# Down projection of a gated ConvFFN: eight block products become seven (Strassen-Winograd), two at a time with the depth outermost

## The chip, the cores and the metric

The kernel runs on one core of a Trainium2 chip. The metric is the device time of one execution in microseconds (us). The names of the engines are those of the profile: PE is the matrix engine (PEld its weight loads), DVE the vector engine, ACT the scalar engine, POOL the general engine, SP the engine whose queue issues all DMAs here. SBUF is the memory on the core, PSUM the accumulators' memory, of 8 banks of 128x512 fp32 numbers.

## The reference

The reference is one layer of a decoder with three sub-layers: two token mixers side by side, cross-attention to 256 memory tokens, and a gated ConvFFN. Each is normalised before and after (RMSNorm) and added to the residual stream. There are 1024 tokens, 1024 features, and 2816 hidden features in the ConvFFN. The change is in the last product and what follows it:

```python
def conv_ffn(h, w_up, conv_w, conv_b, w_down):
    a = causal_depthwise_conv(h @ w_up, conv_w, conv_b)
    val, gate = jnp.split(a, 2, axis=-1)
    return (val * jax.nn.gelu(gate)) @ w_down        # (1024 x 2816) @ (2816 x 1024)
...
        f = conv_ffn(h, w_up[l], conv_w[l], conv_b[l], w_down[l])
        x = x + rmsnorm(f, g_ffn_post[l])
```

## The kernel before

Everything is kept with features on the partitions and tokens along the free axis; tokens come in two halves of 512, h = 0 and h = 1. An fp32 product is made of three fast products: each operand is split into a rounded part and a rest (`hi`, `lo`), and `mm3` (L227) issues hi x hi, hi x lo and lo x hi into one bank. So each 128x512 operand costs an ACT cast (`hi`) and a DVE subtraction (`lo`), in `split` (L250) for activations and in `Stream.split_to` (L117) for weights, which are loaded as 128x512 tiles tagged `raw`.

The gated hidden features come out of the up projection as 22 blocks of 128 (`NP`), for each token half, and are written to DRAM (`fd[k][h]`, L1215). The up projection is itself done by Strassen's scheme in its second part; its last products are those of block 21, in the order of `TURN` (L61): S2, S1, S3, 22 and S4.

`down` (L1346) then computes the output's 8 feature blocks of 128. `sweep(h, done)` (L1352) takes one token half: for each of the 22 depth blocks it loads the hidden block (`get_f`, L1337), splits it, and adds three matmuls to each of seven banks. The eighth block has no bank during the sweep. `last` (L1366) computes it afterwards from the hidden parts that are still in SBUF, in one go for h = 0 and by two quarters of 256 tokens for h = 1. The first half's statistics and output (`finish`, L755) run beside the second sweep, a step at a time. The second half ends by quarters: statistics of the first quarter (`rms`, L273) and their broadcast (`bcast`, L300) are taken while the last quarter's matmuls run (`steps1`, at the depth blocks `TAIL_R` and `TAIL_B`), and its output is finished by `finish_pair` (L771) on DVE and POOL. After the last matmul come the square, the statistics, the broadcast and the output of the last quarter.

`rms` has PE sum the squares over partitions (L278), then 11 small DVE operations for the inverse root; `bcast` has PE spread the result (L305) and ACT copy it to SBUF (L308).

A scheduler sets the order of each engine's instructions when the program is built: it simulates the program and takes the ready instruction that was written first. Each engine then works through its own list in order, and waits at an instruction until that one's inputs are there and its buffer is free. From `self.pinned = True` (L1424) on, marked instructions keep the program's order among themselves; those that are not marked (those of `finish` are not) go where the simulation finds them ready. Buffers have tags with a fixed number of slots (L54 to L58): `w` 13 (weight parts), `b` 32, `raw` 4, `f` 20, `fr` 4, `rs` 4.

## Time and profile before

| | us |
|---|---|
| median of three timed runs (lowest, highest) | 1372.89 (1370.04, 1375.63) |
| the profiled execution | 1373.9 |
| its span, first to last instruction | 1372.2 |
| last matmul of the last product ends, in the span | 1355.8 |
| PE busy, share of the span | 1301.2 (95%) |
| DVE, ACT, POOL busy | 979.4, 618.6, 543.3 |
| mean granted PE clock | 0.971 |

A row of a timeline gives the start, the length, the engine, the line of the kernel, the operation, output <- inputs, shapes and count; in brackets stands how long the engine had waited and for what. "x24" merges 24 instructions in a row. A row of stretches gives, from A to B, each engine's busy time and count, the PE clock, the DMA engines' busy share and the rate in GB/s.

### The profile page before, as it was taken

How to read it: one execution, taken by the hardware profiler on the slowest of the kernel's cores; microseconds unless marked ns; L12 is line 12 of the kernel's file. 1: busy time of each engine (PE TensorE's matmuls, PEld its weight loads, DVE VectorE, ACT ScalarE, POOL GpSimd, SP SyncE). 2: the span in 40 equal slices, each digit the busy share in tenths (PEclk: the TensorE clock that was granted, in tenths of full speed). 3: DMA queues.
4: the chain of work that ended last, by engine and by line, in shares of the span. 5: the costliest groups of instructions: out<-in, count | busy, mean ns of one | idle time of the engine just before them, and what ended most of it. 6: DMA issues, size and time to landing. Idle time of an engine off the chain costs nothing. (4 is left out here: it accounts for less than half of the span.)

```text
span 1372.2 us, 19095 instructions
## 1 busy us (share of the span) xinstructions
PE 1301.2 (95%) x6418; PEld 1100.4 (80%) x6418; DVE 979.4 (71%) x1605; ACT 618.6 (45%) x1155; POOL 543.3 (40%) x433
## 2 busy tenths in 40 slices
PE   9799898779998999889999999999999999999995
PEld 8688897778887888778887788888888888887885
DVE  7968788876376547785577978888898884257225
ACT  7223331245444445444545545555555564253232
POOL 1576345834245005530544568666564110020002
PEclk9899999889999999999999999999999999999997
DMA  9644326346335214442376685545453176356431
GB/s 314 188 145 133 94 72 174 88 140 199 99 119 161 68 48 131 154 154 70 102 231 213 193 279 172 161 154 164 143 169 122 60 251 206 96 149 220 144 114 62
DMA packets 136259, 204.20 MB, mean 149 GB/s; under 512 B 32096, under 2 KB 47328, under 8 KB 136160
## 3 DMA queue, kind: packets, MB, share of 16 engines
q1 hardware_dynamic: 136160, 202.98, 47.8%
q8 instruction: 50, 0.82, 0.3%
q14 instruction: 49, 0.40, 0.1%
HBM read 156.41 MB, written 42.32 MB: 145 GB/s over the span
## 5 line engine op out<-in xcount | busy, mean ns | idle before, releaser
L233 PE MATMUL acc<-b,w 128*128 128x512 f32 (+1 forms) x2496 | 593.7, 391 | 7.7 <-DVE b L730 4.0
L233 PEld LDWEIGHTS acc<-b,w 128*128 128x128 f32 x2496 | 465.0, 191 | 104.6 <-DVE b L730 6.1
L134 DVE TENSOR_TENSOR w<-raw,w 128x512 fp32r<-128x512 f32 (+2 forms) x306 | 261.4, 860 | 208.5 <-PE acc L233 129.3
L131 ACT CAST w<-raw 128x512 fp32r<-128x512 f32 x328 | 198.3, 607 | 242.4 <-PE acc L233 129.3
L233 PE MATMUL sx<-b,w 128*128 128x512 f32 x912 | 220.8, 393 | 1.9 <-ACT T L1275 1.9
L233 PEld LDWEIGHTS sx<-b,w 128*128 128x128 f32 x912 | 172.9, 190 | 38.5 <-ACT T L1275 2.3
L710 POOL TENSOR_TENSOR ac<-ac,sq 128x512 f32<-128x512 f32 x49 | 74.9, 1537 | 289.5 <-ACT sq L709 246.2
L233 PE MATMUL acc<-T,w 128*128 128x512 f32 x528 | 127.0, 389 | 0.0
L233 PEld LDWEIGHTS acc<-T,w 128*128 128x128 f32 x528 | 99.1, 188 | 20.5
L724 POOL TENSOR_TENSOR m<-m,rs 128x512 f32<-128x512 f32 x32 | 50.1, 1570 | 61.4 <-DMA rs<-x1d 17.0
L233 PE MATMUL sx<-T,w 128*128 128x512 f32 x264 | 66.5, 389 | 0.0
L233 PEld LDWEIGHTS sx<-T,w 128*128 128x128 f32 x264 | 49.6, 188 | 10.3
L709 ACT ACTIVATE sq<-m 128x512 f32<-128x512 f32 x63 | 39.6, 632 | 28.3 <-POOL m L724 14.2
L774 POOL TENSOR_TENSOR m<-m,st 128x512 f32<-128x512 f32 x3 | 4.8, 1591 | 117.9 <-ACT st L308 117.9
L233 PE MATMUL acc<-w,b 128*128 128x256 f32 x384 | 50.9, 290 | 0.0
L1214 POOL TENSOR_TENSOR b<-b,m 128x512 f32<-128x512 f32 x22 | 31.5, 1434 | 46.1 <-ACT m L1213 45.7
L233 PEld LDWEIGHTS acc<-w,b 128*128 128x128 f32 x384 | 48.4, 197 | 0.1
L115 POOL TENSOR_TENSOR st<-st,b 128x512 f32<-128x512 f32 x20 | 26.4, 1319 | 54.3 <-DMA st<-in_w_up 39.2
L134 DVE TENSOR_TENSOR w<-b,w 128x512 fp32r<-128x512 f32 x40 | 42.1, 1052 | 7.7 <-issue 4.9
L134 POOL TENSOR_TENSOR w<-raw,w 128x512 fp32r<-128x512 f32 x22 | 30.4, 1383 | 41.8 <-ACT w L131 22.7
L723 DVE SCALAR_TENSOR_TENSOR m<-m,gains,st 128x512 f32<-128x512 f32 x32 | 38.3, 1262 | 5.6 <-ACT st L308 5.6
L1200 ACT ACTIVATE m<-acc,conv 128x512 f32<-128x512 f32 x44 | 34.4, 782 | 15.1 <-DVE acc L1319 11.9
(333 smaller groups left out, 2056.8 us busy)
## 6 DMA issues: line engine op xcount, KB each, us to landing
raw<-in_w_up SPq DMA_DIRECT2D x68, 256.0 KB, 2.9
raw<-in_w_dk SPq DMA_DIRECT2D x44, 256.0 KB, 2.7
fr<-fd SPq DMA_DIRECT2D x41, 256.0 KB, 4.0
b<-in_w_up SPq DMA_DIRECT2D x40, 256.0 KB, 2.8
raw<-in_w_dk SPq DMA_DIRECT2D x44, 192.0 KB, 2.5
raw<-in_w_out SPq DMA_DIRECT2D x32, 256.0 KB, 2.7
raw<-in_w_q SPq DMA_DIRECT2D x32, 256.0 KB, 2.8
raw<-in_w_o SPq DMA_DIRECT2D x32, 256.0 KB, 2.7
```

Of the source, the lines that this page charges most:

```text
L115: g.tensor_tensor(p["S4"], p["12"], p["S2"], ALU.subtract)
L131: nc.scalar.copy(hi[:, :w], t[:, :w])
L134: e.tensor_tensor(lo[:, :w], t[:, :w], hi[:, :w], ALU.subtract)
L233: self.pin(nc.tensor.matmul(ps, lhsT=x, rhs=y, start=first and i + j == 0, stop=last and i == n - 1 and j == 2, skip_group_check=go_on))
L709: nc.scalar.activation(sq, src, AF.Square)
L710: (e or nc.gpsimd).tensor_tensor(acc, acc, sq, ALU.add)
L723: v.scalar_tensor_tensor(x, x, self.gain[gpost][:, i:i + 1], bc, ALU.mult, ALU.mult)
L724: g.tensor_tensor(x, x, rs, ALU.add)
L774: self.pin(e.tensor_tensor(x, x, bc, ALU.mult))
L1200: nc.scalar.activation(t, src, AF.Identity, bias=self.cw(blk, 3), scale=self.cw(blk, 2))
L1214: nc.gpsimd.tensor_tensor(val, val, gate, ALU.mult)
```

## The change

The output's features are cut into two halves of four blocks, the tokens into their halves, and the depth of 22 blocks into two halves of 11 (k and k + 11). Winograd's form of Strassen's scheme makes the 2x2 block product from seven products of 11 depth blocks. They are done in four phases; in the first three, two products run at a time in 2 x 4 banks (`A` and `B`), with the depth outermost:

- Phase 0: weights "11" by hidden "a" into A, "12" by "b" into B. Their sum is the final x11 (first four feature blocks, second token half).
- Phase 1: S2 by T2, added on into A, and S1 by T1 into B anew.
- Phase 2: S3 by T3, added on into A, and S4 by "d" added on into B. What A and B hold at the ends of phases 1 and 2 is combined on ACT and DVE into x12 and x22 (all eight blocks of the first token half).
- Phase 3: weights "22" by T4, added on into A, which then holds the last four blocks of the second token half. It runs by quarters: all 11 depth steps for 256 tokens, then for the other 256 tokens block by block.

S1 to S4 are sums and differences of weight blocks, T1 to T4 of hidden blocks. They are made per depth step by `d_sums` on 128x512 tiles: T1 on DVE, the others on POOL. Each is then split like any operand. T2 and S2 stay in SBUF until T4 and S4 are made from them. `d_prep` keeps loads, sums and splits ahead of the matmuls; the shared weight stream no longer serves this product.

A depth step of phases 0 to 2 has 24 matmuls of 512 columns, 4 splits and 4 or 5 loads of 256 KB. Phase 1 adds 3 sums on POOL and one on DVE per step, phase 2 adds 3 on POOL, and phase 3 one on POOL. In all there are 33 x 24 = 792 matmuls of 512 columns and 264 of 256, where before there were 990 and 132.

The first token half's squares, statistics and output (`first_half`) can start only after phase 2, and so run beside phase 3; the quarters' statistics are placed at `TAIL_R` = (0, 7) and `TAIL_B` = (1, 4), which are block and depth step of the last quarter.

```diff
-TAIL_R = 5
-TAIL_B = 10
+TAIL_R = (0, 7)
+TAIL_B = (1, 4)
 T_FROM = 11
 T_RATE = 1
 FETCH = 2
-OUT_RATE = 1
-F_AHEAD = 3
-F_FIRST = {"S1": 1, "S3": 2, "22": 3}
+D_LOAD = 2
+D_FIRST = {"S3": 1, "22": 2}
 SLOTS = {"b": 32, "m": 16, "w": 13, "st": 3, "ac": 2, "sq": 2, "raw": 4}
 SLOTS_1 = {"k": 15, "x": 14}
 SLOTS_2 = {"kv": 16, "t": 11, "rs": 2}
 SLOTS_3 = {"T": 24, "rs": 2, "t": 3}
-SLOTS_4 = {"f": 20, "fr": 4, "rs": 4}
+SLOTS_4 = {"f": 21, "fr": 4, "rs": 4}
 BANKS = {"acc": 4, "sx": 3, "st": 1}
...
-        for h in range(2):
-            for k in range(NP):
-                ids["dn"][h, k] = [w.add(a["w_dk"][k][:, c:c + n].unsqueeze(1)) for c, n in ((0, 512), (512, 384))]
-            ids["d7"][h] = [w.add(a["w_d7"][:, k:min(k + 4, NP)]) for k in range(0, NP, 4)]
...
-                if i == NP - 1 and name in F_FIRST:
-                    self.get_f(F_FIRST[name], "t")
+                if i == NP - 1 and name in D_FIRST:
+                    self.d_prep(D_FIRST[name])
...
-    def get_f(self, n, tag="fr"):
-        while len(self.f) < min(n, 2 * NP):
-            h, k = divmod(len(self.f), NP)
-            t = self.slot(tag)
-            self.nc.sync.dma_start(t, self.fd[k][h])
-            hl = self.f[h, k] = self.pair("b" if 0 <= k - 4 * h < 16 else "f")
-            self.split(*hl, t)
+    def d_load(self, n):
+        nc = self.nc
+        ph, k = divmod(n, 11)
+        s = self.ds[k]
+        def get(key, src, tag):
+            s[key] = self.slot(tag)
+            nc.sync.dma_start(s[key], src)
+        w = lambda o, j: self.a["w_dk"][k + 11 * j][:, HALF * o:HALF * o + HALF]
+        x = lambda j, h: self.fd[k + 11 * j][h]
+        if ph == 0:
+            get("11", w(0, 0), "b")
+            get("12", w(0, 1), "raw")
+            get("a", x(0, 1), "t" if n < 2 else "f")
+            get("b", x(1, 1), "t" if n < 2 else "fr")
+        elif ph == 1:
+            if k < 2:
+                get("a", x(0, 1), "f")
+            get("21", w(1, 0), "f")
+            get("22", w(1, 1), "b")
+            get("c", x(0, 0), "f")
+            get("d", x(1, 0), "f")
+        elif ph == 2:
+            get("11", w(0, 0), "b")
+            get("21", w(1, 0), "f")
+            get("12", w(0, 1), "raw")
+            get("c", x(0, 0), "f")
+            get("d", x(1, 0), "f")
+        else:
+            get("22", w(1, 1), "raw")
+            get("b", x(1, 1), "fr")
+    def d_sums(self, n):
+        v, g = self.nc.vector, self.nc.gpsimd
+        ph, k = divmod(n, 11)
+        s = self.ds[k]
+        def sub(key, to, x, y, e=g, op=ALU.subtract):
+            e.tensor_tensor(s[to], s[x], s[y], op)
+            s[key] = s[to]
+        if ph == 1:
+            sub("S1", "22", "21", "22", g, ALU.add)
+            sub("S2", "11", "S1", "11")
+            sub("T1", "c", "c", "a", v)
+            sub("T2", "a", "d", "T1")
+        elif ph == 2:
+            sub("S3", "21", "11", "21")
+            sub("S4", "S2", "12", "S2")
+            sub("T3", "c", "d", "c")
+        elif ph == 3:
+            sub("T4", "b", "b", "T2")
+    def d_split(self, n):
+        ph, k = divmod(n, 11)
+        s = self.ds[k]
+        names = (("11", "a", "12", "b"), ("S2", "T2", "S1", "T1"), ("S3", "T3", "S4", "d"), ("22", "T4"))[ph]
+        for i, key in enumerate(names):
+            if i % 2 == 0:
+                tag = "w" if ph < 3 or k < 6 else "b"
+            else:
+                tag = "b" if ph < 3 or k >= 8 else "f"
+            hl = self.dp[n, i] = self.pair(tag)
+            self.split(*hl, s.pop(key) if key not in ("S2", "T2", "11", "a", "d") else s[key])
+    def d_prep(self, n):
+        while self.n_prep < min(n, 44):
+            i = self.n_prep
+            while self.n_load <= min(i + D_LOAD, self.d_last):
+                self.d_load(self.n_load)
+                self.n_load += 1
+            while self.n_sums <= min(i + 1, 43):
+                self.d_sums(self.n_sums)
+                self.n_sums += 1
+            self.d_split(i)
+            self.n_prep += 1
+    def d_begin(self):
+        self.ds = [{} for _ in range(11)]
+        self.dp = {}
+        self.n_load = self.n_sums = self.n_prep = 0
+        self.d_last = 1
     def down(self):
...
+        nc = self.nc
         v, g = nc.vector, nc.gpsimd
+        self.d_last = 43
+        A = [self.bank() for _ in range(4)]
+        B = [self.bank("sx" if b < 3 else "st") for b in range(4)]
+        col = lambda b: slice(b * P, b * P + P)
+        x11, x12, x22 = [], [], []
+        p1, sq = x11, [self.slot("ac"), self.slot("ac")]
         quarters = [slice(0, 256), slice(256, 512)]
         wide = lambda x: x[:, :256].unsqueeze(1).to_broadcast([P, 2, 256])
         mg, res = [[], []], [[], []]
+        def out_part(b, q, src):
+            if b % 2 == 0:
+                mg[q].append(self.slot("m", shape=[P, 2, 256]))
+                res[q].append(self.slot("b", shape=[P, 2, 256]))
+            nc.sync.dma_start(res[q][-1][:, b % 2], self.x2d[b][1][:, quarters[q]])
+            self.pin(nc.scalar.activation(mg[q][-1][:, b % 2], src, AF.Identity,
+                                          scale=self.gain["g_ffn_post"][:, b:b + 1]))
+        def ready(ph, n, b, ps):
+            if ph == 0 and n == 0:
+                x11.append(self.slot("m"))
+                nc.scalar.copy(x11[b], ps)
+            elif ph == 0:
+                v.tensor_tensor(x11[b], x11[b], ps, ALU.add)
+            elif ph == 1:
+                t = self.slot("m")
+                nc.scalar.copy(t, ps)
+                (x22 if n else x12).append(t)
             else:
+                t = (x12 if n else x22)[b]
+                v.tensor_tensor(t, t, ps, ALU.add)
+        for n in range(33):
+            ph, k = divmod(n, 11)
+            self.d_prep(n + 3 + max(0, n - 27))
+            for i, banks in enumerate((A, B)):
+                wt, xs = self.dp.pop((n, 2 * i)), self.dp.pop((n, 2 * i + 1))
+                new = ph == 0 or (ph == 1 and i == 1)
+                for b in range(4):
+                    self.mm3(banks[b], [(wt[0][:, col(b)], wt[1][:, col(b)], *xs)], ticks=0, first=new and k == 0,
+                             last=k == 10, go_on=not new)
+                    if k == 10:
+                        ready(ph, i, b, banks[b])
+            if ph == 1 and k < 4:
+                self.sumsq(x11[k], sq[1], k == 0)
+            if ph == 2 and k < 8:
+                out_part(k // 2, k % 2, x11[k // 2][:, quarters[k % 2]])
+        m = x12 + x22
+        B = None
+        def first_half():
+            for b in range(8):
+                self.sumsq(m[b], sq[0], b == 0, v)
+                if b % 2:
+                    yield
+            yield from self.finish(m, sq[0], 0, self.x2d)
+        job = first_half()
+        parts = []
+        def one(k, b, c):
+            wt, xs = parts[k]
+            self.mm3(A[b][:, c], [(wt[0][:, col(b)], wt[1][:, col(b)], xs[0][:, c], xs[1][:, c])], ticks=0,
+                     first=False, last=k == 10, go_on=True)
+        def squares(b, q):
+            c = quarters[q]
+            s = self.slot("sq")[:, :256]
+            self.pin(nc.scalar.activation(s, A[b][:, c], AF.Square))
+            self.pin(v.tensor_tensor(sq[1][:, c], sq[1][:, c], s, ALU.add))
+        for k in range(11):
+            self.d_prep(44 if k > 5 else 39 + k)
+            parts.append((self.dp.pop((33 + k, 0)), self.dp.pop((33 + k, 1))))
+            for b in range(4):
+                one(k, b, quarters[0])
+                if k == 10:
+                    squares(b, 0)
+                    out_part(4 + b, 0, A[b][:, quarters[0]])
+            next(job, None)
+        self.drain(job)
         self.pinned = True
         st = {}
+        for b in range(4):
+            for k in range(11):
+                one(k, b, quarters[1])
+                if (b, k) == TAIL_R:
+                    st["r"] = self.rms(sq[1][:, quarters[0]], 2)
+                if (b, k) == TAIL_B:
+                    bc = self.bcast(st["r"], 2)[1]
+                    for i in (3, 2):
+                        self.drain(self.finish_pair(mg[0][i], res[0][i], wide(bc), i, 1, 0, g))
+                    st["out"] = self.chain(*(self.finish_pair(mg[0][i], res[0][i], wide(bc), i, 1, 0, v)
+                                             for i in (0, 1)))
+                if (b, k) > TAIL_B and k % 3 == 0:
+                    next(st["out"], None)
+            if b == 3:
+                self.drain(st["out"])
+            squares(b, 1)
+            out_part(4 + b, 1, A[b][:, quarters[1]])
+        r = self.rms(sq[1][:, quarters[1]], 2)
         ps, bc = self.bcast(r, 2)
...
```

The order of the instructions is shown at three places. Line numbers are those of each program: L304, L277, L765, L766, L280 and L1494 now are what was L305, L278, L766, L767, L281 and L1416 before, and L1374 is `d_sums`. Buffer numbers follow the tags.

On PE, in the last quarter, this stood between the last quarter's statistics and broadcast in the program before (the ends of that piece, which is a run of L233 matmuls):

```order
L278 MATMUL st<-ones,ac_11867 128x1 x2
L233 MATMUL acc<-b_12086,w_12727 128x256
...
L233 MATMUL acc<-b_12249,w_12743 128x256
L305 MATMUL st<-ident,rs_y_12938 128x128 x2
L233 MATMUL acc<-b_12288,w_12742 128x256
```

And so it stands now, with the first half's broadcast (x4) just ahead of the quarter's statistics (L277), and 24 matmuls between these and the quarter's broadcast (L304, x2):

```order
L304 MATMUL st<-ident,rs_y_12811 128x128 x4
L277 MATMUL st<-ones,ac_10861 128x1 x2
L232 MATMUL acc<-b_12745,b_12741 128x256
...
L232 MATMUL acc<-f_12585,w_12582 128x256
L304 MATMUL st<-ident,rs_y_12987 128x128 x2
L232 MATMUL acc<-f_12622,w_12618 128x256
```

The first half's broadcast, which before stood in the middle of the second sweep, now stands between the two quarters' statistics.

On DVE, at the same place, before: the quarter's square, then its statistics, then its output.

```order
L1416 TENSOR_TENSOR ac_11867<-ac_11867,sq_12911 128x256
L281 TENSOR_SCALAR st_x<-st 128x2
L261 TENSOR_SCALAR rs_y_12938<-st_x 128x2
...
L270 SCALAR_TENSOR_TENSOR rs_y_12938<-rs_t_12939,rs_y_12938 128x2
L774 TENSOR_TENSOR m_12749<-m_12749,st_12968 128x512
```

Now the 8 scalings (L765) and the 8 residual additions (L766) of the first half stand ahead of the quarter's statistics (first and last of each are shown):

```order
L269 SCALAR_TENSOR_TENSOR rs_y_12811<-rs_t_12812,rs_y_12811 128x4
L765 SCALAR_TENSOR_TENSOR m_12000<-m_12000,gains,st_12860 128x512
...
L765 SCALAR_TENSOR_TENSOR m_12035<-m_12035,gains,st_12860 128x512
L766 TENSOR_TENSOR m_12000<-m_12000,rs_12788 128x512
...
L766 TENSOR_TENSOR m_12035<-m_12035,rs_12802 128x512
L280 TENSOR_SCALAR st_x<-st 128x2
L260 TENSOR_SCALAR rs_y_12987<-st_x 128x2
```

So the quarter's inverse root, which PE's broadcast reads, comes behind those 16 operations in DVE's list.

On POOL, before, this product had only squares to add up, seven of the first row's kind, and then a part of the quarters' outputs:

```order
L710 TENSOR_TENSOR ac_10866<-ac_10866,sq_11864 128x512
L774 TENSOR_TENSOR m_12827<-m_12827,st_12968 128x512
L776 TENSOR_TENSOR m_12827<-m_12827,rs_12828 128x512
L774 TENSOR_TENSOR m_12799<-m_12799,st_12968 128x512
L776 TENSOR_TENSOR m_12799<-m_12799,rs_12800 128x512
```

Now it has 77 sums (L1374) and 4 additions of squares. Here is the piece from S1 of step 18 (k = 7, into b_11599) to S2 of step 18 (into b_11022):

```order
L1374 TENSOR_TENSOR b_11599<-f_11597,b_11599 128x512
L1374 TENSOR_TENSOR b_11654<-f_11652,b_11654 128x512
L1374 TENSOR_TENSOR f_11814<-f_11816,f_11814 128x512
L709 TENSOR_TENSOR ac_10861<-ac_10861,sq_11649 128x512
L1374 TENSOR_TENSOR b_10926<-raw_12098,b_10926 128x512
L1374 TENSOR_TENSOR b_11706<-f_11704,b_11706 128x512
L1374 TENSOR_TENSOR b_11022<-b_11599,b_11022 128x512
```

Between the two stand S1 of steps 19 and 20 (b_11654, b_11706), the first T3 of phase 2 (f_11814), a square, and the S4 that phase 2 needs at its sixth step (b_10926).

More of the change, by code (lines that the diff above doesn't have):

```diff
@@ L1346, in down @@
     def down(self):
-        nc, w, ids = self.nc, self.w, self.ids
+        nc = self.nc
         v, g = nc.vector, nc.gpsimd
-        f, get = self.f, self.get_f
-        def sweep(h, done):
-            ps = [self.bank("acc" if b < 4 else "sx") for b in range(7)]
-            for k in range(NP):
-                get(h * NP + k + F_AHEAD)
-                hl = [w.get(i) for i in ids["dn"][h, k]]
-                for b in range(7):
-                    c = slice(b % 4 * P, b % 4 * P + P)
-                    hi, lo = hl[b // 4]
-                    self.mm3(ps[b], [(hi[:, c], lo[:, c], *f[h, k])], ticks=0, first=k == 0, last=k == NP - 1)
-                    if b in (3, 6):
-                        self.tick()
-                    if k == NP - 1:
-                        done(b, ps[b])
@@ L1439, in down @@
-        ps = self.bank()[:, :256]
-        last(1, ps, quarters[1], steps1)
-        self.drain(st["out"])
-        done1(7, ps, (1,))
-        r = self.rms(acc[:, quarters[1]], 2)
+        for b in range(4):
[15 more added lines that the diff above has]
+            out_part(4 + b, 1, A[b][:, quarters[1]])
```

65 lines of the change are left out of this document (3 added, 62 removed).

## The prediction

> **What bounds the kernel now.** I read the busy times first, then the stretches from the end of the up projection on, then the timeline at the ends of that part.
>
> ```profile
> PE 1301.2 (95%) x6418; PEld 1100.4 (80%) x6418; DVE 979.4 (71%) x1605; ACT 618.6 (45%) x1155; POOL 543.3 (40%) x433
> ...
> 1100.00:1150.00 50.00, 50.00 (x222) 41.44 (x221) 38.13 (x64) 30.47 (x54) 5.69 (x4) 1.00 0.83 277
> 1150.00:1200.00 50.00, 50.00 (x223) 41.40 (x222) 13.21 (x21) 12.28 (x22) 0.00 (x0) 1.00 0.36 98
> 1200.00:1250.00 50.00, 49.11 (x224) 40.44 (x223) 29.70 (x49) 29.36 (x54) 10.94 (x7) 1.00 0.53 159
> 1250.00:1300.00 50.00, 50.00 (x222) 41.36 (x221) 23.25 (x37) 11.90 (x21) 0.00 (x0) 1.00 0.58 185
> 1300.00:1340.00 40.00, 40.00 (x185) 33.41 (x184) 12.09 (x19) 14.46 (x30) 0.00 (x0) 1.00 0.38 108
> 1340.00:1373.00 33.00, 17.55 (x135) 16.82 (x133) 18.01 (x38) 5.64 (x14) 9.57 (x6) 0.78 0.19 64
> ```
>
> In the down projection PE never stops (one idle of 0.89 us), its clock is 1.00, and POOL and mostly DVE are free. So this stage costs what its matmuls cost, and every matmul less is time won, unless another engine or a wait takes its place. The pace of PE:
>
> ```profile
> 1066.30 5.44 PE acc L233 x24
> ...
> 1339.67 5.92 PE L233 MATMUL acc<-b,w 128*128 128x256 f32 x48
> ```
>
> 24 matmuls of 512 columns take 5.44 us (0.2267 each); 48 of 256 take 5.92 less the last one's overlap of 0.16, that is 0.120 each. The quarters' shape costs 6% over half a long one.
>
> **The matmuls.** Before: 990 x 0.2267 + 132 x 0.120 = 224.4 + 15.8 = 240.3. Now: 792 x 0.2267 + 264 x 0.120 = 179.5 + 31.7 = 211.2. **-29.1 us**. The counts stand in the program's order, so that the work shrinks is certain. All else is what may eat it.
>
> **The sums: POOL and DVE share something.** Phases 1 and 2 put 3 POOL sums on each depth step of 5.44 us, and 5 or 4 DVE operations of two SBUF inputs. In the trace the two engines slow each other:
>
> ```profile
> 656.48 5.14 POOL L253 TENSOR_TENSOR b<-m,b 128x512 fp32r<-128x512 f32 x3
> 658.70 1.77 DVE L134 TENSOR_TENSOR w<-raw,w 128x512 fp32r<-128x512 f32 x1
> 660.40 1.77 DVE L253 TENSOR_TENSOR b<-m,b 128x512 fp32r<-128x512 f32 x1
> 666.21 1.89 DVE L134 TENSOR_TENSOR w<-raw,w 128x512 fp32r<-128x512 f32 x3
> 675.20 1.29 POOL L710 TENSOR_TENSOR ac<-ac,sq 128x512 f32<-128x512 f32 x1 [2.45 <-ACT sq L709]
> 676.45 1.29 POOL L134 TENSOR_TENSOR w<-raw,w 128x512 fp32r<-128x512 f32 x1
> ```
>
> Alone, DVE takes 0.69 and starts one each 0.605 (1.89 for three); POOL takes 1.29 and starts one each 1.25. With both busy, each starts one every 1.70 (658.70 to 660.40). So a POOL sum takes 1.70 - 0.605 = 1.095 us of DVE's time away. A step of phase 1 needs 3 x 1.095 + 5 x 0.605 = 6.31 and one of phase 2 3 x 1.095 + 4 x 0.605 = 5.71, both more than PE's 5.44. A step of phase 0 has no sums and needs 2.42, and POOL may work ahead there. How far, the order tells: when PE begins phase 1 (59.8 us after its first product), I put POOL at the 20th of its 80 operations, since T1 on DVE and the buffers of S2 let it no further. From there to the last step of phase 1 (step 21, where PE is due 54.4 us later) 32 POOL and 39 DVE operations come first in the lists: 32 x 1.095 + 39 x 0.605 + 1.0 for the cast before the split = 59.6. DVE reaches that place in its list some 2 us before PE begins the phase (with the first finished bank of B), so 56.4 us are there. **+3.2 us**. Bounds: 0 if POOL gets further ahead; without any lead (6.31 - 5.44) x 11 + (5.71 - 5.44) x 11 = 12.5. I am nearer to the lead because the order has sums of steps 11 to 15 before PE starts phase 1.
>
> The Trainium skill, "SBUF — State Buffer", section "Who interferes with whom", says of this pair that it is an exclusive lock: a DVE instruction with two SBUF inputs and a POOL one that reads SBUF exclude each other for the whole instruction. The trace has less: a pair takes 1.70, not 1.29 + 0.69 = 1.98. By the rule the term would be 32 x 0.28 = 9.0 larger, 12 instead of 3.
>
> **Loads.** 4 to 5 loads of 256 KB per step are 193 to 241 GB/s, where the stretch 1100 to 1150 has 277. They land in 2.7 to 4.0 us,
>
> ```profile
> raw<-in_w_dk SPq DMA_DIRECT2D x44, 256.0 KB, 2.7
> fr<-fd SPq DMA_DIRECT2D x41, 256.0 KB, 4.0
> ```
>
> and are issued two steps (10.9 us) ahead of the splits. I take 0; if each sum waited a load's time the lead would go, which is the case of 12.5 above. The start costs nothing either: the first two steps are split during the up projection's last block, as three hidden blocks were before.
>
> **The first half's statistics (phase 3).** Between the end of phase 2 and the first half's statistics, DVE has 8 additions, 9 splits and 7 squares' additions: 24 x 0.69 = 16.6 us. It can begin 2.7 early (bank A is done 12 matmuls before B), and one weight load of 2.7 is exposed, as `raw` has four slots. So 16.6 us against 124 x 0.120 = 14.9 of PE: **+1.7** (0 at 0.605 apiece; 5 with a second load).
>
> **The second statistics' wait.** PE's broadcast of the first quarter's root stands 24 matmuls behind the first half's broadcast, and DVE's root behind the first half's 16 output operations. Those rows in the trace:
>
> ```profile
> 1248.15 1.13 PE L305 MATMUL st<-ident,rs_y 128*128 128x128 f32 x8
> 1249.31 0.59 ACT L308 COPY st<-st 128x512 f32<-128x512 f32 x1 [0.23 <-PE st L305]
> 1249.93 4.73 DVE L766 SCALAR_TENSOR_TENSOR m<-m,gains,st 128x512 f32<-128x512 f32 x7 [0.83 <-ACT st L308]
> L767 DVE TENSOR_TENSOR m<-m,rs x8: 683/688/693, 1255.8 to 1263.9; 128x512 f32<-128x512 f32 x8
> 1261.96 0.69 DVE L767 TENSOR_TENSOR m<-m,rs 128x512 f32<-128x512 f32 x1 [0.77 <-DMA rs<-x2d]
> 1360.52 0.16 DVE L281 TENSOR_SCALAR st_x<-st 128x2 f32<-128x2 f32 x1 [1.11 <-PE st L278]
> 1362.79 0.77 PE L305 MATMUL st<-ident,rs_y 128*128 128x128 f32 x2 [2.31 <-DVE rs_y L270]
> ```
>
> Broadcast to first scaling 1.78; 8 scalings at 0.664 (4.73 less 0.75, over six) 5.3; the eight additions took 8.1 from first to last start with three splits between, and still wait for residuals, whose four slots `rs` come free only as the first four additions end, so I take 7.0 + 0.69; the root 2.27 (1360.52 to 1362.79). Together 17.0 after the broadcast. PE has its own work for 5.2 of it: the statistics can start when ACT has copied (1.75), they take 0.5, and 24 matmuls 2.9. PE then stands for **+11.8 us**: queued behind the broadcast in PE's list are the 84 last matmuls, and the end waits for those. Bounds: with eight additions at 0.605 the wait is 9; with 8.1 it is 13. Nothing in DVE's list can move the root ahead, so no gain at this place; only a list other than the one built would.
>
> **The clock after the wait.** Such a wait has a row:
>
> ```profile
> 257.41 0.79 PE L616 MATMUL sx<-x,x 128*128 128x127 f32 x2 [7.00 <-DVE x L605]
> 250.00:257.00 7.00, 0.41 (x2) 0.00 (x0) 5.85 (x7) 0.81 (x2) 5.59 (x5) 0.68 0.52 150
> 257.00:264.00 7.00, 6.59 (x25) 5.91 (x26) 5.19 (x6) 2.48 (x5) 7.00 (x6) 0.59 0.41 112
> ```
>
> After 7.0 us of idle PE worked 6.59 us at a mean clock of 0.59: 6.59 x 0.41 = **+2.7** (0 to 5: none, or twice that after the longer idle).
>
> **The tail.** From the last matmul to the last statistics:
>
> ```profile
> 1354.88 0.88 PE L233 MATMUL acc<-f,w 128*128 128x256 f32 x6
> 1355.80 0.47 ACT L1409 ACTIVATE m<-acc,gains 128x256 f32<-128x256 f32 x1 [3.58 <-PE acc L233]
> 1357.94 1.48 DVE L1416 TENSOR_TENSOR ac<-ac,sq 128x256 f32<-128x256 f32 x1
> 1359.47 1.01 PE L278 MATMUL st<-ones,ac 128*128 128x1 f32 x4 [3.71 <-DVE ac L1416]
> ```
>
> 3.71 us, because ACT scaled (0.47) before it squared and DVE still shared with POOL the first quarter's output. Now the square comes first, and that output is done earlier by the length of the matmuls still to come (84 x 0.120 = 10 us). What is left is about 1.0: **-2.7** (0 if the output is as late as before).
>
> **The sum.** -29.1 + 3.2 + 1.7 + 11.8 + 2.7 - 2.7 = -12.4. The profiled execution took 1373.9 (span 1372.2), so 1361.5 for it and 1360 for the span; the runs' median of 1372.9 lies 1.0 below the profiled one, which gives **1360.5 us**.
>
> **Rivals.**
>
> Forecast, 0.47: gain 6 to 20 us, 1353 to 1367.
>
> *The second wait isn't there* (0.20): PE comes to its broadcast later than I put it, or the additions run through with their residuals loaded. Then the 11.8 and 2.7 go: 1346. For it: `rs` loads are short; against it: the list has the 16 operations ahead in any case, 10 us by their own rows.
>
> *Ports without a lead* (0.18): POOL and DVE bind in phases 1 and 2 at the trace's pairs: +12.5 for +3.2, 1370, no difference that can be told. For it: POOL's list mixes sums that aren't due for ten steps with those due next (an S4 or T3 ahead of S2 of step 18).
>
> *Ports as a full lock, and no lead* (0.15), the slower side: a pair costs 1.98. A step of phase 1 then takes 3 x 1.98 + 2 x 0.605 = 7.15 and of phase 2 3 x 1.98 + 0.605 = 6.55, so (1.71 + 1.11) x 11 = 31 for 3.2: 1388. It decides for slower once the mean step of the two phases exceeds 5.44 + (12.4 + 3.2) / 22 = 6.15 us. Against it: the 1.70 of the rows. The Trainium skill's rule above is this one's first half.
>
> That PE has no less to do is excluded by the count.
>
> **How the numbers follow.** About 0.5% (6.9 us) is what a measurement of this kernel can tell from no change, so faster is below 1366.0 and slower above 1379.8. Faster: most of the forecast (0.41), all of the case without the wait (0.20): 0.61. Same: the rest of the forecast 0.06, the ports without a lead 0.17: 0.23. Slower: 0.15 and 0.01 of the case before: 0.16. The range leaves out half of the full-lock case and the lowest tenth: 1345 to 1378; the forecast's own is 1353 to 1367.
>
> **What would show it.** PE busy about 29 us lower in sum over the stage; rows of PE waiting on L304 for DVE's L269 of 9 to 13 us, once, then a stretch of clock near 0.6; in phase 1 POOL over 70% busy with sums of 1.6 us and DVE operations of 1.7 beside them, and PE waits on S2 or T2 splits of some us in all; a last L277 about 1 us behind the last matmul. Wrong is the forecast if PE stands much during phase 0 (loads), if the waits in phases 1 and 2 exceed 12 us, or if the wait at L304 is under 5.

## The result: slower by 0.6%, and the profile after

The changed kernel takes 1381.4 us (median of 13 runs, 1377.1 to 1384.8) against 1373.2 us for the kernel before on the same chip (13 runs). The ratio is 1.0057, with a 95% interval of 1.0042 to 1.0073: slower, where the prediction had 1360.5. The profiled execution took 1384.1 us, 2.8 more than the median; its span is 1382.4 us (before 1372.2).

Busy times of the kernel after, from its page:

```profile
PE 1281.1 (93%) x6352; PEld 1084.1 (78%) x6352; DVE 1064.7 (77%) x1645; ACT 627.3 (45%) x1172; POOL 662.5 (48%) x506
```

PE has 66 matmuls and 20 us less. That is less than the 29 predicted, since matmuls at a low clock cost it about 9 us, as shown below. DVE has gained 85 us and POOL 119.

The four longest waits of PE in the kernel after, from 1090 us on (us in total, how often, the longest):

```profile
PE st L304 <- DVE rs_y L269: 14.8, 2, 12.5
PE acc L232 <- ACT m L1450: 11.0, 1, 11.0
PE acc L232 <- ACT m L1445: 4.6, 1, 4.6
PE acc L232 <- DVE w L252: 2.4, 1, 2.4
```

The first row holds the wait that was predicted (12.5; the other 2.3 is the last quarter's). The second and third are new: PE waits for ACT's copies of bank A at the ends of phase 1 and phase 0. The fourth, 2.4 us for a split in phase 1, is all that PE waits for splits of the sums.

Busy times by stretch (stretch, its length, then PE, its weight loads, DVE, ACT and POOL, each with its count, then PE's granted clock, the DMA share and GB/s):

```profile
1113.00:1173.00 60.00, 60.00 (x266) 49.57 (x264) 52.09 (x58) 27.70 (x49) 33.62 (x21) 1.00 0.85 297
1173.00:1178.00 5.00, 0.37 (x3) 0.13 (x1) 5.00 (x4) 1.28 (x3) 4.37 (x4) 0.90 0.88 263
1178.00:1185.00 7.00, 7.00 (x19) 5.43 (x20) 7.00 (x6) 3.26 (x7) 7.00 (x5) 0.59 0.67 205
1185.00:1220.00 35.00, 34.25 (x150) 27.69 (x149) 35.00 (x25) 12.43 (x23) 35.00 (x21) 1.00 0.48 156
...
1223.20:1228.00 4.80, 4.76 (x14) 3.81 (x15) 4.09 (x4) 2.18 (x4) 4.64 (x3) 0.66 0.89 305
...
1257.50:1264.50 7.00, 7.00 (x21) 5.54 (x22) 5.41 (x6) 7.00 (x16) 4.55 (x3) 0.66 0.56 183
1264.50:1319.70 55.20, 55.20 (x245) 45.72 (x244) 38.76 (x47) 26.07 (x49) 20.58 (x13) 1.00 0.35 113
...
1357.20:1363.00 5.80, 5.80 (x33) 5.80 (x34) 3.19 (x4) 1.12 (x3) 4.06 (x3) 0.65 0.24 88
```

Phase 0 (up to 1173) and phase 2 from 1264 on run as predicted, with PE full. From 1173 to 1220 DVE is busy without a gap and POOL with one of 0.6 us, and DVE gets through 25 operations in 35 us. Behind each of four waits the clock is 0.59 to 0.66 for 5 to 7 us: 7.00 x 0.41 + 4.76 x 0.34 + 7.00 x 0.34 + 5.80 x 0.35 = 8.9 us lost.

The last statistics follow the last matmul closely:

```profile
1370.71 0.61 PE L277 MATMUL st<-ones,ac 128*128 128x1 f32 x4 [0.93 <-DVE ac L1494]
```

The last matmul ended 0.93 before this, at 1369.8, and 12.6 us before the end of the span (before: 1355.8 and 16.4).

Why do ACT's copies come late? The timeline of the kernel after, on PE, ACT, DVE and POOL, at the ends of phase 0 and of phase 1 (start, length, engine, line; in brackets the idle time before and what ended it):

```profile
1146.62 1.73 POOL L1374 TENSOR_TENSOR fr<-fr,f 128x512 f32<-128x512 f32 x1 [6.18 <-DMA fr<-fd]
1148.82 1.78 DVE L252 TENSOR_TENSOR w<-b,w 128x512 fp32r<-128x512 f32 x1
1150.52 1.78 DVE L252 TENSOR_TENSOR b<-fr,b 128x512 fp32r<-128x512 f32 x1
...
1172.40 0.84 PE L232 MATMUL st<-b,w 128*128 128x512 f32 x3
1176.71 0.62 ACT L251 CAST b<-f 128x512 fp32r<-128x512 f32 x1 [5.18 <-DVE w L252]
1177.24 2.04 ACT L1445 COPY m<-acc 128x512 f32<-128x512 f32 x4
1183.35 0.67 DVE L1447 TENSOR_TENSOR m<-m,sx 128x512 f32<-128x512 f32 x1
...
1255.83 0.62 ACT L251 CAST b<-f 128x512 fp32r<-128x512 f32 x1 [9.00 <-DMA f<-in_w_dk]
1256.87 1.55 ACT L1450 COPY m<-acc 128x512 f32<-128x512 f32 x3
```

PE ends phase 0 at 1173.2 (1172.40 and three matmuls in 0.84). ACT's copies of the finished bank A start at 1177.24, behind a cast for which ACT has stood 5.18 us. At the end of phase 1 ACT stands 9.00 us for one more cast, and the copies come behind that too. What those casts are, ACT's list of the changed program shows (row number, line, output and input). At the end of phase 1, which is step 21:

```
1001 L251 CAST w_11936<-b_10737 128x512
1002 L251 CAST b_12054<-f_11921 128x512
1003 L251 CAST b_12062<-f_11923 128x512
1004 L251 CAST w_11981<-f_11864 128x512
1005 L251 CAST b_12111<-f_11974 128x512
1006 L251 CAST w_11989<-b_10745 128x512
1007 L251 CAST b_12119<-f_11976 128x512
1008 L251 CAST w_12050<-f_11917 128x512
1009 L1450 COPY m_12000<-acc 128x512
```

b_12111 and b_12119 are the T3 and "d" of step 25, w_12050 is S3 of step 24. They stand ahead of the copies without which PE can't start step 22, three steps (16 us) before it needs step 25. ACT's 9.00 us are for b_12119, which waits for its load. At the end of phase 0 (step 10) it is the T2 of step 14 in the same way. The scheduler takes what its simulation finds ready, so it had these casts ready early. On the chip they were late, because the splits before them were late and held the buffers into which the loads go. SP's queue, which issues the loads, shows that from 1225 to 1262 us:

```profile
SPq L1342 <- DVE b L252: 20.7, 9, 6.2
```

Nine loads waited there for subtractions of splits on DVE (L252), 20.7 us in all.

### The profile page after: what moved, and what is told of

It reads as the page before. It is cut to its first block, busy times and chain, and to the rows that moved or that the text cites. A ratio compares the mean times of both kernels' runs of the same rounds, so it can differ in the third digit from the quotient of the medians.

```text
span 1382.4 us, 19079 instructions
## 1 busy us (share of the span) xinstructions
PE 1281.1 (93%) x6352; PEld 1084.1 (78%) x6352; DVE 1064.7 (77%) x1645; ACT 627.3 (45%) x1172; POOL 662.5 (48%) x506
## 5 line engine op out<-in xcount | busy, mean ns | idle before, releaser
L232 PE MATMUL acc<-b,w 128*128 128x512 f32 x2412 | 593.9, 399 | 26.1 <-ACT m L1450 11.0
L133 DVE TENSOR_TENSOR w<-raw,w 128x512 fp32r<-128x512 f32 x206 | 194.3, 950 | 102.1 <-PE acc L232 72.8
L232 PE MATMUL sx<-b,w 128*128 128x512 f32 x921 | 223.7, 392 | 2.0 <-ACT T L1270 1.9
L130 ACT CAST w<-raw 128x512 fp32r<-128x512 f32 x228 | 141.4, 622 | 121.6 <-PE acc L232 69.7
L709 POOL TENSOR_TENSOR ac<-ac,sq 128x512 f32<-128x512 f32 x45 | 68.8, 1538 | 184.7 <-ACT sq L708 141.5
L252 DVE TENSOR_TENSOR b<-f,b 128x512 fp32r<-128x512 f32 x53 | 66.8, 1267 | 10.8 <-ACT b L251 10.5
L252 DVE TENSOR_TENSOR w<-b,w 128x512 fp32r<-128x512 f32 x44 | 57.3, 1305 | 6.6 <-PE acc L232 4.3
L251 ACT CAST b<-f 128x512 fp32r<-128x512 f32 x53 | 32.3, 619 | 64.0 <-DVE w L252 45.1
L1374 POOL TENSOR_TENSOR f<-f,f 128x512 f32<-128x512 f32 x22 | 36.0, 1637 | 17.2 <-DMA f<-fd 12.4
```

Source lines behind the costliest of these rows:

```text
L130: nc.scalar.copy(hi[:, :w], t[:, :w])
L133: e.tensor_tensor(lo[:, :w], t[:, :w], hi[:, :w], ALU.subtract)
L232: self.pin(nc.tensor.matmul(ps, lhsT=x, rhs=y, start=first and i + j == 0, stop=last and i == n - 1 and j == 2, skip_group_check=go_on))
L251: self.nc.scalar.copy(hi, src)
L252: (e or self.nc.vector).tensor_tensor(lo, src, hi, ALU.subtract)
L709: (e or nc.gpsimd).tensor_tensor(acc, acc, sq, ALU.add)
```

## Experiments

All kernels below compute the whole result. A time is a median; the ratio is to the kernel before on the same chip, with its 95% interval, and microseconds worked out between two experiments come from ratios (0.0010 is 1.37 us), since the runs come from several chips. By the intervals such a difference is good to some 3 us either way, and to 5 or 6 where e5, e6 or e7 is one of the two. Code is cut to what matters; "..." stands for the rest. S, T and bank names are those of the change.

| run | time, us | ratio to before |
|---|---|---|
| the change | 1381.4 | 1.0057 (1.0042 to 1.0073) |
| e1: broadcast late | 1377.4 | 1.0034 (1.0015 to 1.0052) |
| e2: copies first | 1372.6 | 0.9997 (0.9981 to 1.0012) |
| e3: sums on DVE | 1357.4 | 0.9894 (0.9874 to 0.9914) |
| e4: e1 + e2 + e3 | 1352.1 | 0.9861 (0.9838 to 0.9883) |
| e5: e3, residuals early | 1350.0 | 0.9836 (0.9804 to 0.9867) |
| e6: e3, root first | 1346.5 | 0.9805 (0.9765 to 0.9845) |
| e7: e5 + e6 | 1346.4 | 0.9803 (0.9772 to 0.9834) |
| e8: e3, idle operations on POOL | 1379.3 | 1.0045 (1.0028 to 1.0063) |
| e9: early sums on DVE | 1374.1 | 1.0006 (0.9994 to 1.0018) |
| e10: e7, tail without POOL | 1344.7 | 0.9789 (0.9765 to 0.9814) |
| e11: e9, copies first | 1371.3 | 0.9979 (0.9961 to 0.9997) |
| e12: e10, last outputs held back | 1345.0 | 0.9777 (0.9760 to 0.9793) |
| e13: only the casts out of turn moved | 1370.7 | 0.9980 (0.9965 to 0.9995) |
| e14: e9 + e13 | 1366.3 | 0.9945 (0.9926 to 0.9963) |

### The sums on DVE (e3)

```diff
         def sub(key, to, x, y, e=g, op=ALU.subtract):
-            e.tensor_tensor(s[to], s[x], s[y], op)
+            v.tensor_tensor(s[to], s[x], s[y], op)
```

> All sums of the down projection on DVE, none on POOL; ACT's list stays within a row or two of what it was. The shared port as the cause of the late casts: POOL no longer takes 1.095 us of DVE per sum, DVE needs 8 x 0.605 = 4.84 us for a step of phase 1 and 7 x 0.605 = 4.24 for one of phase 2, both under PE's 5.44, so the waits at 1178 and 1223 go (4.6 + 2.4 and 4.5 of slow clock) and most of that at 1257: 1360 to 1370. The loads as the cause: slots come free no earlier, the wait at the end of phase 1 stays at 9 to 11: about 1370. ACT's order alone as the cause, whatever the sums take: all waits stay, 1379 to 1383. DVE then the bottleneck (it has every sum and every split in one list): slower than 1383.

Measured: 1357.4 us, 22.4 us less than the change by the ratios, and 2.6 below the first range (1360 to 1370). All that PE waits for from 1090 us on in this kernel:

```profile
PE st L304 <- DVE rs_y L269: 14.9, 2, 12.6
PE st L277 <- DVE ac L1494: 0.9, 1, 0.9
PE st L277 <- ACT st L307: 0.8, 1, 0.8
```

Every wait at the ends of phases 0 and 1 and inside phase 1 is gone, with ACT's list within three rows of what it was. At the end of phase 1 the same casts still stand ahead of the copies; at the end of phase 0 the cast of step 14's T2 has moved behind three of the four. So ACT's order costs nothing at the end of phase 1 as long as the casts come in time, and the loads aren't the cause: the same loads with the same slots were in time here. The same 45 us of phase 1 in the change and then in e3 (columns as above; DVE's is the third, POOL's the fifth):

```profile
1180.00:1225.00 45.00, 41.87 (x173) 33.37 (x173) 44.31 (x33) 14.87 (x28) 43.67 (x27) 0.96 0.52 167
```

```profile
1180.00:1225.00 45.00, 45.00 (x200) 37.28 (x199) 42.39 (x70) 20.41 (x37) 10.75 (x3) 1.00 0.66 212
```

DVE alone does 70 operations in 42.4 us, 0.605 each. Beside POOL it does 33 in 44.3. POOL's 27 in this stretch make 60 for both engines together, ten fewer than DVE does by itself. Handing these sums to POOL made the two together slower.

### POOL beside DVE without the dependence (e8)

Sums on DVE, and POOL reads each sum of the weights once more, into a buffer that nothing reads:

```diff
             s[key] = s[to]
+            if key[0] == "S":
+                g.tensor_tensor(self.dm, s[to], s[to], ALU.add)
...
+        self.dm = self.slot("rs")
```

> Sums on DVE (1357.4 alone), and for each of the 44 sums of the weights one operation on POOL that reads the sum and writes a buffer that nothing reads: no split waits for POOL. The shared port as the cause: each of the 44 takes 1.095 us of DVE's time, a step of phase 1 needs 2 x 1.095 + 8 x 0.605 = 7.03 and one of phase 2 2 x 1.095 + 7 x 0.605 = 6.43, so PE waits on splits or copies come back: (1.6 + 1.0) x 11 = 28 us without any lead, 15 with one like before, time 1370 to 1390. If what mattered was that splits had to wait for sums made by another engine: 1357 to 1360.

Measured: 1379.3 us, 20.7 us more than e3 by the ratios, inside the 15 to 28 expected for POOL beside DVE. The list of every engine is that of e3, in the same order, but for the 44 operations. No split waits for POOL here, and PE waits in phases 0 to 2 again:

```profile
PE acc L232 <- ACT m L1453: 11.3, 1, 11.3
PE acc L232 <- DVE w L252: 2.6, 3, 1.3
PE st L232 <- DVE m L1450: 1.9, 1, 1.9
```

With 2.3 us more in shorter ones these are 18.1 us, where the change has 18.7. The wait at the end of phase 1 is back nearly as it was. The wait for the copies at the end of phase 0 is not; bank additions and splits stand in its place. POOL doesn't hold a buffer back either: no load waits for it, and DVE waits for it once, 0.9 us. So it is POOL's work beside DVE that costs, not that a split waits for another engine's result. e3 changes two things with a sum, where it is made and what runs beside it; e8 puts one of them back.

### Copies first (e2, e11)

At step 10 and step 21 the casts of the step after next are written behind the copies, and all casts of the next four steps may only be issued behind them:

```diff
-            self.d_prep(n + 3 + max(0, n - 27))
+            with self.tc.issue_after(copied[0].ins) if copied and k < 4 else nullcontext():
+                self.d_prep(n + 3 + max(0, n - 27), k < 10 or ph == 2)
 ...
+            if k == 10 and ph < 2:
+                with self.tc.issue_after(copied[0].ins):
+                    self.d_prep(n + 3)
```

> Only ACT's list at the ends of phases 0 and 1 is another: the copies of the finished banks come ahead of the casts for the steps after next (with the casts and splits of these queued behind). ACT's order as the cause: PE's waits on the copies (4.6 and 11.0 us) go and with them the slow clock after them (2.9 and 2.4), 20.9 us in all, time 1360.5. The shared port of DVE and POOL as the cause: both are busy without a break from 1149 to 1247, so PE only comes to wait on splits of steps 13 to 21 instead (the wait at 1223 grows from 2.4 to about 9 us), the second wait goes: about 1370. The loads as the cause: the casts of steps 23 and 24 were waiting for loads that landed at 1255.8, so PE waits at these steps instead of at the copies: 1376 to 1382.

Measured: 1372.6 us, 2.6 above the second expectation. The waits on the copies are gone, and waits for splits have come instead, most of them in phase 1, as that one said (the longest is 4.3 us, not 9). The two rows of them, and ACT's first copies in this kernel:

```profile
PE acc L232 <- DVE w L252: 9.2, 5, 4.3
PE sx L232 <- DVE w L252: 2.3, 2, 1.3
...
1166.64 2.63 ACT L1447 COPY m<-acc 128x512 f32<-128x512 f32 x4 [8.22 <-PE acc L232]
```

ACT now stands 8.22 us for PE with casts behind it that it could have done. The edit did more than it was meant to, so it can't divide the loss between ACT's list and POOL's work beside DVE. The same edit on e9 (below) has the same flaw:

> The run with the early sums on DVE (1374.1: splits in time, but 9.4 us of PE's wait for ACT's copies at the end of phase 1) and ACT's copies first. If the order of ACT's list is the second, separate cause, and there only because casts for steps 23 and 24 wait: that wait goes with its 2.4 us of slow clock, 1362 (1360 to 1365). If the sums of phase 2 on POOL or their loads are late in themselves, PE waits for splits of steps 22 to 25 instead: 1368 to 1374.

Measured: 1371.3 us, in the range of the second expectation, but not for its reason: PE's waits for splits rise from 2.6 to 11.5 us, all before 1233 us and so inside phase 1, not at steps 22 to 25. The edit needed to be cut down, which e13 and e14 do.

### The lost start (e9)

The prediction let DVE begin phase 1's part of its list 2 us before PE's phase 1. The row L1447 above has it at 1183.35, 10 us after PE's 1173.2. POOL had started 19 of its 80 operations (77 sums and 3 additions of squares) by the end of phase 0, close to the 20th that the prediction assumed, but from 1146 on each had held DVE up. Here the sums of steps 11 to 14, which POOL had made in phase 0, and those of phase 3 are made on DVE. The program has 54 of the 77 left on POOL, not 51 of 88 as the two expectations count:

```diff
+            e = v if n < 15 or n > 32 else e
             e.tensor_tensor(s[to], s[x], s[y], op)
```

> The change as it is, but the sums of steps 11 to 14 and those of phase 3 on DVE; those of steps 15 to 32 stay on POOL (51 of the 88 that POOL had). POOL's first 19 sums ran beside phase 0 and held DVE's splits up, so that DVE came to the first addition of a bank of B at 1183.4, where the forecast had 1171. If that lost start is why the forecast's 3.2 us for the sums became 24: DVE is there at 1172 to 1174, no wait at the end of phase 0, waits of phase 1 and its end together 3 to 6 us, time 1360 to 1366. If the pairs in phases 1 and 2 themselves are too dear whatever the start: waits of 12 us or more stay at the end of phase 1, 1370 to 1377.

Measured: 1374.1 us. PE's waits in phases 0 and 1, and DVE's first addition of a bank of B:

```profile
PE acc L232 <- ACT m L1451: 9.4, 1, 9.4
PE sx L232 <- DVE m L1448: 2.4, 1, 2.4
PE acc L232 <- DVE w L252: 2.3, 2, 2.1
PE sx L232 <- DVE w L252: 0.3, 1, 0.3
...
1173.36 1.87 DVE L1448 TENSOR_TENSOR m<-m,sx 128x512 f32<-128x512 f32 x3
```

DVE is there at 1173.4, as expected, and the splits cost 2.6 us. But 9.4 us at the end of phase 1 stay: the lost start is not the whole of it. The time lies 8 us above the first range and inside the second, whose sign was a wait of 12 us or more there.

### Only the casts out of turn (e13, e14)

The first part of the edit above alone: casts of step 13 and later (24 and later) are issued behind A's copies, and those up to step 12 (23) stay ahead.

```diff
-            self.d_prep(n + 3 + max(0, n - 27))
+            with self.tc.issue_after(copied[0].ins) if copied and k < 4 else nullcontext():
+                self.d_prep(n + 3 + max(0, n - 27))
...
```

The scheduler lets the other engines' lists follow: on DVE, four subtractions of steps 13 and 14 (casts moved here) now stand behind the first addition of a bank of B instead of ahead of it.

> The change with POOL's sums as they are, and of ACT's list only this moved: casts of step 13 and later (24 and later) may no longer stand ahead of the four copies of bank A at the end of step 10 (21); all casts up to step 12 (23) stay ahead, so ACT doesn't stand idle for the copies. If the casts out of turn cost what PE waited for the copies: -4.6 -2.9 -11.0 -2.4, of which the sums' late start (12 us on DVE) takes back up to 9 at splits of phase 1: 1365 to 1372, splits waited for 8 to 12 us. If the earlier run with the copies first (1372.6) showed all that the order can give: 1371 to 1374.

> The same edit on the run whose early sums are on DVE (1374.1; splits waited for 2.6 us, a bank's addition 2.4, the copies at the end of phase 1 9.4). If the 9.4 is ACT's order alone, it goes with its slow clock: 1362 (1360 to 1365), and this with 51 sums left on POOL. If the sums of phase 2 are late in themselves beside POOL, PE waits for steps 22 to 24 instead: 1369 to 1374.

Measured: 1370.7 us on the change (e13) and 1366.3 us with the early sums on DVE (e14). PE's waits for splits and bank additions in e13 (one of 0.3 us left out), then in e14:

```profile
PE acc L232 <- DVE w L252: 5.1, 6, 2.0
PE sx L232 <- DVE w L252: 3.4, 4, 1.7
PE sx L232 <- DVE m L1447: 2.5, 2, 2.2
```

```profile
PE acc L232 <- DVE w L252: 3.2, 4, 2.0
PE sx L232 <- DVE w L252: 1.5, 4, 0.4
PE sx L232 <- DVE m L1448: 0.4, 2, 0.3
PE st L232 <- DVE m L1448: 0.3, 1, 0.3
```

The waits on the copies are gone in both. In e13 8.5 us for splits and 2.8 for bank additions take their place (expected 8 to 12), in e14 4.7 and 0.7, spread over phase 1 in pieces of 0.1 to 0.4 us and one of 2.0. The time of e13 is inside its first expectation. That of e14 is 4 us above its own (1.3 above the range), yet its waits are not at steps 22 to 24, so neither wording fitted it: DVE and POOL don't keep up with PE in phase 1 itself. By the ratios, the 22 us between the change and e3 divide like this: ACT's list 10.6 (change to e13), the lost start 4.8 (e13 to e14), the sums beside the splits in phases 1 and 2 themselves 7.0 (e14 to e3). Made in the other order, the start is worth 7.0 (change to e9) and the list 8.4 (e9 to e14), which the 3 us either way can't tell from the first. The two aren't quite apart either: in e13, with POOL's early sums as they were, DVE reaches the first addition of a bank of B at 1173.36 too, so the four subtractions ahead of it were a part of the 10 us. All three parts are there only because POOL's sums and DVE's operations slow each other, as e3 shows.

### The second statistics' wait (e1, e5, e6)

```diff
-TAIL_B = (1, 4)
+TAIL_B = (3, 0)
```

> One constant: the broadcast of the first quarter's root (PE L304) stands 26 block steps instead of 8 behind the root's own matmuls, so 54 of the 84 last matmuls (6.5 us at 0.120) come ahead of the wait for DVE. If that wait is what the last stretch costs (root ready at 1357.2, PE standing 12.5 us, then 84 matmuls): wait about 6 us, last matmul 6.5 us earlier, time 1375 (1373 to 1377). Rival, the end is set by the first quarter's output on POOL and DVE, which now falls together with the last quarter's statistics: the tail behind the last matmul grows from 12.7 to 17 or more and the time is 1379 to 1382.

Measured: 1377.4 us, 3.2 less than the change by the ratios and 0.4 above the first range. PE's waits from 1330 us on:

```profile
PE st L304 <- DVE rs_y L269: 8.5, 2, 6.2
PE st L277 <- DVE ac L1494: 2.6, 1, 2.6
```

The wait halves to 6.2 as worked out. 1.7 us come back at L277, where the last squares now stand behind the first quarter's output on DVE, and the tail behind the last matmul grows from 12.6 to 14.8. Theory and rival each have a part.

In e5 the first half's residuals get eight slots instead of four (`self.slot("rs")` becomes `self.slot("b")` in `finish`), on top of e3:

> Sums on DVE as before this run (1357.4), and the first half's residuals in eight buffers of b in place of four of rs, so that they are loaded before they are needed. The second statistics' wait was 12.6 us, of which DVE stood 3.5 us for loads of rs between the eight additions. If those loads are a part of the wait as the rows say: wait 9.1 (16 operations at 0.605 to 0.67, and the root), time 1354. If the order of DVE's list alone sets it and the loads lie beside other work: wait 12.6 still, 1357.

Measured: 1350.0 us. The wait falls from 12.6 to 8.7 us, as expected, and the time is 4 below the 1354. It fell by 8 us with an interval of about 5 either way, where the wait accounts for 3.9. The profiled spans differ by 5.0, of which 1.0 was there before the down projection, in which alone the two programs differ; so the trace shows no gain beyond the wait.

In e6, on top of e3, DVE's first-half output operations (L765, L766) may be issued only behind the root:

```diff
+                if (b, k) >= TAIL_R and k % 3 == 1:
+                    with self.tc.issue_after(self.root.ins):
+                        next(job, None)
...
```

> Sums on DVE, and in DVE's list the second root ahead of the first half's 16 output operations. If these operations ahead of the root are the whole of the wait: the wait on L304 falls from 12.6 to under 1 us and with it about 2 us of slow clock, the last matmul ends 14 us earlier. What of it reaches the end hangs on DVE, which then has the 16 operations beside the last quarter: if they fit (10.4 us of them and 2.6 for the first quarter's output against 10 us of matmuls and 3 behind) 1344 to 1347; if DVE becomes the bound of the tail, 1350 or more; if the wait has another cause, 1357.

Measured: 1346.5 us, 12.2 less than e3 by the ratios. The wait for the second root is gone, and a new one stands at the last statistics, since DVE isn't done with the output. PE's two longest waits from 1290 us on in e6:

```profile
PE st L278 <- DVE ac L1496: 8.5, 1, 8.5
PE st L305 <- DVE rs_y L269: 2.3, 1, 2.3
```

DVE had work for the whole tail, and the order only decides what waits for it. The waits account for 7.1 us: 12.6 and 2.0 of slow clock are gone, and the last wait grew from 0.9 to 8.5. The profiled spans differ by 9.8, of which 2.7 was there before the down projection. That leaves 7.1; the 12.2 of the ratios, good to 6 either way, is no sign of more. DVE bounds the tail here, as the second wording had it, yet the time lies in the first range.

### Less for DVE in the tail (e4, e7, e10, e12)

> The three together: broadcast late, copies first, sums on DVE. If the causes are the order of ACT's list with the port behind it, and the second statistics' wait apart from both, the gains add up to the three waits in phases 0 and 1 (18.0) with their clock (6.9) and 6.5 of the last: 1350 (1346 to 1355), and below the kernel before. If loads are behind it: 1362 to 1368. If the gains are the same microseconds seen twice, no less than the best of the three.

Measured: 1352.1 us: the gains of e1 and e3 add up, and with the sums on DVE the copies' order adds nothing that can be told.

> The two together: root first and the residuals in eight buffers. The 3.5 us for which DVE stands for loads should now count only if DVE bounds the tail: then 3 us below the run with the root first alone, otherwise the same time within 1 us. 1342 to 1346.

Measured: 1346.4 us, 0.4 above the range; the last wait falls from 8.5 to 6.7, and the time, within its interval, not at all.

In e10 the first quarter's output is made on DVE alone (`g` becomes `v` in `finish_pair`'s call):

> Sums on DVE, root first and residuals in eight buffers (1346.4), and the first quarter's output on DVE alone: four operations fewer on POOL in the tail. There the eight scalings on DVE took 9.5 us beside POOL, 5.4 without. The shared port: 4 x 1.095 for 4 x 0.605, DVE is done 2.0 us earlier, the wait for the last statistics (6.7) falls to about 4.7 and the time to 1344.5. If POOL's operations are help rather than load there: four more operations of 0.6 to 0.7 in DVE's list, 1348.5 to 1349.

Measured: 1344.7 us. DVE's eight scalings of the first half in e6, beside POOL, and in e10, without, and then e10's wait:

```profile
1313.48 9.54 DVE L767 SCALAR_TENSOR_TENSOR m<-m,gains,st 128x512 f32<-128x512 f32 x8
```

```profile
1313.98 5.39 DVE L767 SCALAR_TENSOR_TENSOR m<-m,gains,st 128x512 f32<-128x512 f32 x8
...
PE st L278 <- DVE ac L1496: 5.0, 1, 5.0
```

DVE takes over four operations and is done earlier: POOL slows DVE in this stage too. (e7 has the same 9.54 as e6.) The time is 1.9 us below e7 by the ratios, too little to be told. In e12 the last two pairs of the first half's output go behind the last root:

> The fastest so far (1344.7: sums on DVE, root first, residuals early, the tail without POOL) with the last two of the first half's eight pairs of output operations behind the last root on DVE. DVE stands 1.8 us there for the broadcast. 4 operations of 0.61 come off the wait for the last statistics (5.0), 0.6 of them come back ahead of the last output: 1343 (1342 to 1344.5). If the end hangs on the last stores and not on DVE: 1344.7.

Measured: 1345.0 us, no difference from e10 that can be told, though the wait fell from 5.0 to 2.5; 1.0 of it came back behind the root. The 1343 and the 1344.7 expected lie too close to choose between. e10 and e12 are 2.1 to 2.2% faster than the kernel before (29 to 31 us).

## Why the prediction was wrong

- **The matmuls (-29.1)**: right. PE's busy time fell by 20.1 us, and 8.9 went to the low clock, 29.0 together. With the sums on DVE and the tail in order, the kernel gains 29 to 31 us over the one before (e10, e12); that this is the same number is chance, since the tail has terms of its own. In the change as made, the time went elsewhere.
- **The sums (+3.2, bounds 0 to 12.5): the step that failed.** They cost 22.4 us (the change against e3). The pair's price was right: 1.70 us in 1148.82 to 1150.52, and e8's 20.7 us lies within what it gives. Two things were wrong in its use. First, "DVE reaches that place in its list some 2 us before PE begins the phase" was read as if POOL's early sums in phase 0 were free; the pairs ran from 1146 on, and DVE was there 10 us after PE, in part because of four subtractions that the list had ahead of that place. The step had priced the pairs in phases 1 and 2 only. Second, it asked only when splits would be late for PE. It didn't ask what is queued behind a late cast on ACT: the copies that free PE's bank. That is 15.6 us of waiting and 5.3 of slow clock in the trace, for 2.4 and 1.6 at splits. With ACT's list mended alone (e13), the sums cost 11.8 us against e3: about the 12.5 that the prediction gave for no lead at all (good to 3 us). With the early sums on DVE as well (e14) it is 7.0, inside the bounds. The other 10.6 came through ACT's list, which the prediction put at nothing.
- **Loads (0)**: right; e3 has the same loads and no wait. The late loads seen at the end of phase 1 waited for slots that late splits held.
- **The first half's statistics (+1.7, bound 0 below)**: no wait of PE shows there, so 0.
- **The second statistics' wait (+11.8, 9 to 13)**: 12.5, by the mechanism given, and the loads of residuals are a part of it (e5).
- **The clock (+2.7)**: 2.0 behind that wait. Three more waits brought 6.9, which had no term; they are part of what the sums cost.
- **The tail (-2.7)**: the last statistics follow the last matmul as predicted, 0.9 us behind; from the last matmul to the end it is 12.6 us for 16.4, so -3.8.

Without the sums' term the forecast was 1360.5 - 3.2 = 1357.3; e3, where the sums cost PE nothing, measured 1357.4. That it fits so closely is luck, as single terms were off by 1 to 2 us. The prediction's own test for being wrong (waits in phases 1 and 2 above 12 us) came true: 11.0, 2.4 and 0.7 in them, and 4.6 at their start.

Of the rivals, the slower side was named with the right point but the wrong price. From the end of phase 0 (1173.2) to the first quarter's matmuls at 1319.75 PE took 146.5 us, 6.66 for a mean step, above the 6.15 given as the point from which the change is slower. But a pair costs 1.70 and not 1.98; the rest came through ACT's list. The case of ports without a lead had the price of the sums about right, and not ACT's list. The Trainium skill, "SBUF — State Buffer", section "Who interferes with whom", has the contention itself, and e3 and e8 bear it out. Its exclusive lock, taken for the whole length of both instructions, would give 1.98; the measurement decides. The Trainium skill, "Perfetto Trace Analysis", section "Optimizing Scalar/DVE Operations", says that offloading between these two engines might not help. Here the runs go further: it costs 22.4 us.

What remains open: how much of the lost start is POOL's early sums and how much the order of DVE's list, and whether POOL's reading or its writing slows DVE, since each of its operations here does both.

## What to carry to other kernels

Price an offload by what it takes from the engine it is meant to relieve, over the whole time in which it runs, including stages where it seems to run ahead for free: a two-input sum on POOL took 1.095 us of DVE here (1.70 for the pair less 0.605), and 0.605 on DVE itself. When a producer gets later, read each engine's list for what stands behind it that something else needs, the release of PE's banks first. And put the short chain that PE will wait for (a root, a broadcast) ahead of output work on the same engine, then check what that output now delays.

## What the hardware showed that was not expected

A slow clock follows waits of very different length for about the same price. Behind 4.6 us of waiting 2.9 us were lost, behind 11.0 us 2.4, behind 12.5 us 2.0. The Trainium skill, "TensorE: Matmul & The Clock Gate", Part 1, says that the clock halves after an idle window of some 3.4 us and comes back after a busy one, with windows that run freely; that the price doesn't grow with the wait agrees. But waits below that length had it too, at times: behind 2.38 us at 1223 in the change the clock was 0.66 for 4.8 us. There the Trainium skill and the measurement differ, and the measurement decides. Three waits in e11, each with the ten matmuls behind it:

```profile
1194.52 2.60 PE L232 MATMUL acc<-b,w 128*128 128x512 f32 x10 [3.25 <-DVE w L252]
1203.57 4.08 PE L232 MATMUL acc<-b,w 128*128 128x512 f32 x10 [2.64 <-DVE w L252]
1232.40 2.57 PE L232 MATMUL acc<-b,w 128*128 128x512 f32 x10 [2.75 <-DVE w L252]
```

Behind the shortest of the three the matmuls took 4.08 us, at a clock of 0.66 over 4.9 us; behind the other two 2.60 and 2.57, at 1.00. So from the length of a wait of 2 to 3 us alone, it can't be told whether the clock will drop.
